# Row blocks combined as they come, joins of inverses in alternating places of the array, squares of keys from a diagonal

## The chip, the cores and the metric

The kernel runs on one core of a Trainium2 chip. The metric is the device time of one execution in microseconds (us), the median of several executions. Lower is better.

## The reference

One decoder block on `x` of 1024 tokens by 1024 channels, all in float32. The normalized input is multiplied by one wide weight `w_in` and split. Two branches follow, then an output product and an MLP:

```python
# gated DeltaNet branch, 8 heads of 128
qkv = silu(causal_short_conv(g_qkv, conv_w))
gq, gk = l2_normalize(q) * 128 ** -0.5, l2_normalize(k)      # k / sqrt(sum(k * k) + EPS)
lhs = strictly_lower(k_beta @ k.T * decay) + eye             # per chunk
sol = triangular_solve(lhs, [v * beta, k_beta * exp(g_cum)])
state = scan over chunks                                     # recurrence per head
...
# attention branch: an indexer selects 256 keys for each query, softmax over them
merged = sigmoid(gate_a) * o_gdn + sigmoid(gate_b) * o_att
x = x + merged @ w_out
h2 = rms_norm(x, norm_mlp_g)
x = x + square(relu(h2 @ w_mlp_up)) @ w_mlp_down             # 1024 -> 4096 -> 1024
```

## The kernel before

**Order.** All work is written as generators that a small planner on the host (`Weave`, line 2003) interleaves. A generator yields None (wait for its own last operation), a key such as `("ss", tb)` (an event that `wv.done` sets) or an engine's letter (until that engine is free by the planner's costs). The planner takes the ready generator with the lowest priority number and so fixes the order of instructions on each engine; an engine then runs its list in that order. Priority 9 is the filler: `gdense` (dense products of `w_in`, line 721), later `wout` and `mlp`. All instructions are recorded through one helper, so the profile puts them on line 2114; tiles tell them apart. Matmuls of plain float32 have two records each (two passes); transposes and products of the rounded float32r halves have one.

**DeltaNet stage.** The tokens form 8 blocks of 128 and a head's matrices have 8 blocks `b`. `keys(h)` (line 820) needs the squared length of each key. `squares` (line 910) gets it so: TensorE transposes four blocks of `kt` into a PSUM tile `tt`, ScalarE squares each with a sum over its row (tile `gj`); twice for 8 blocks. Then come the root (`rsq_w`, three Newton steps on VectorE), the factors `ck`, and for each half four products of keys with themselves, each scaled by `ck` and by the decay `es` in one VectorE operation (tile `am`). GpSimd inverts the 32x32 diagonal blocks. `join(h)` (line 946) puts the inverses together: small matmuls of 32x32 and then 64x64, each placed in a part of the array by `tile_position=(row, column)`, into a PSUM tile `jj`, with ScalarE copies in between. There are four groups of them for a head: 16 and 24 matmuls of 32x32, then 8 and 8 of 64x64. `scan(h)` (line 1044) follows.

**Between attention and MLP.** Attention goes through row blocks in the order 0, 7, 1, 6, 2, 3, 5, 4, two groups of heads each. `wout` multiplies a merged block by `w_out`, `residual` (line 1397) adds `x`, stores the block and sums its squares. The MLP multiplies in a seven-product scheme over two halves of the rows and two halves of the channels. Its first two products of a column pair, p1 and p2, need the normalized rows of blocks 0 to 3 (`norm2`, line 1424), the other five need sums and differences with blocks 4 to 7 (`norm2b`, line 1587, which transposes them in `columns` and splits them in `rounded`). Eight products p1 and p2 of 12 matmuls stand at the head of the order of products (`SEQ`, line 1501).

Of the kernel before, what the change touches and what calls it, by code (L numbers as in the profile page):

```python
# [9 lines left out]
F32 = mybir.dt.float32  # L10
# [4 lines left out]
AF = mybir.ActivationFunctionType  # L15
# [35 lines left out]
def body(tc, a, out, dbg=None):  # L51
# [48 lines left out]

    def rsq_w(pl, dst, src, n, tag):
        t = pl.tile([P, n], F32, name=tag + "t")
        V_.tensor_scalar(dst.bitcast(I32), src.bitcast(I32), -0.5, float(0x5F3759DF), op0=OP.mult, op1=OP.add)
        for _ in range(3):
            yield
            V_.scalar_tensor_tensor(t, dst, -0.5, src, op0=OP.mult, op1=OP.mult)
            yield
            V_.tensor_tensor(t, t, dst, op=OP.mult)
            yield
            V_.scalar_tensor_tensor(dst, t, 1.5, dst, op0=OP.add, op1=OP.mult)  # L110
# [709 lines left out]
    def keys(h):  # L820
# [12 lines left out]
        kss = gp.tile([P, NB], F32, name="kss", bufs=2)  # L833
        yield from squares(kt, kss)
        yield dma
        for b in range(NB):
            A_.activation(es[:, b, :], es[:, b, :], AF.Abs, bias=ngc[:, b, h:h + 1])
            if b % 2:
                yield
            if b % 4 == 3:  # L840
                A_.activation(es[:, b - 3:b + 1, :], es[:, b - 3:b + 1, :], AF.Exp, scale=-1.0)
        rk = gp.tile([P, NB], F32, name="rk", bufs=2)
        ke = gp.tile([P, NB], F32, name="ke", bufs=2)
# [12 lines left out]
        V_.scalar_tensor_tensor(nb_, ck, -1.0, eg[:, :, h], op0=OP.mult, op1=OP.mult)  # L856
        for half in range(2):
            yield tt.ready
            ps, slot_ = tt.get()
            for i in range(4):  # L860
                b = half * 4 + i
                PE_.matmul(ps[:, i, :], blk(kt, b), blk(kt, b), start=True, stop=True)
            yield
            for i in range(4):
                b = half * 4 + i
                V_.scalar_tensor_tensor(am[:, b, :], ps[:, i, :], ck[:, b:b + 1], es[:, b, :],
                                        op0=OP.mult, op1=OP.mult)
                if i % 2:
                    yield
            tt.free(slot_)  # L870
        for half in range(2):
# [74 lines left out]
    def join(h):  # L946
# [8 lines left out]
        ys = am[:, :, 96:128]  # L955
        yp = pj_.tile([P, NB, 32], F32, name="jj")
        for p_ in range(2):
            lo_, hi_ = slice(64 * p_, 64 * p_ + 32), slice(64 * p_ + 32, 64 * p_ + 64)
            for b in range(NB):
                PE_.matmul(yp[lo_, b, :], am[hi_, b, lo_], um[hi_, b, hi_], start=True, stop=True,  # L960
                           tile_position=(64 * p_ + 32, 64 * p_))
        yield
        for p_ in range(2):
            lo_ = slice(64 * p_, 64 * p_ + 32)
            A_.activation(ys[lo_], yp[lo_], AF.Copy)
        yield
        xp = pj_.tile([P, NB, 32], F32, name="jj")
        for p_ in range(2):
            lo_ = slice(64 * p_, 64 * p_ + 32)
# [18 lines left out]
        A_.activation(y6, yp[0:64], AF.Copy)  # L988
        yield
        xp = pj_.tile([P, NB, 64], F32, name="jj")  # L990
        for b in range(NB):
            PE_.matmul(xp[0:64, b, :], t64[0:64, b, :], y6[:, b, :], start=True, stop=True, tile_position=(0, 0))
        yield
        A_.activation(um[0:64, :, 64:128], xp[0:64], AF.Copy, scale=-1.0)
        yield
# [379 lines left out]
    def wout():  # L1375
        yield ("drained", last, 1)
        for idx, (qb, g) in enumerate(ATT):
# [15 lines left out]
            if g:  # L1393
                wv.add(1, residual(qb, pw))
        wv.done("wout")
# [18 lines left out]
    def norm_out(half, k, ps, ring, slot_):  # L1414
# [6 lines left out]
        wv.done("h2k", half, k)  # L1421


    def norm2():
        for tb in range(4):
            yield ("ss", first * 4 + tb)
        bs = slice(first * 4, first * 4 + 4)
        V_.tensor_scalar(nms[:, bs], nss[:, bs], 1.0 / D, EPS, op0=OP.mult, op1=OP.add)
        yield
        yield from rsq_w(cst, nr[:, bs], nms[:, bs], 4, "n2")  # L1430
        yield
        for tb in range(4):
            yield ("xd", first * 4 + tb)
        for c in range(2):
            ys = [x1[first * 4 + i][:, c * HALF:(c + 1) * HALF] for i in range(4)]
            for i in range(4):
                V_.tensor_scalar(ys[i], ys[i], nr[:, first * 4 + i:first * 4 + i + 1], None, op0=OP.mult)
            yield
            for k in range(4 * c, 4 * c + 4):
                ring = (ss, ptr)[k % 2]  # L1440
                yield ring.ready
                ps, slot_ = ring.get()
                for i in range(4):
                    PE_.transpose(ps[:, i * P:(i + 1) * P], ys[i][:, (k % 4) * P:(k % 4 + 1) * P], ident)
                wv.add(1, norm_out(first, k, ps, ring, slot_))

    wv.add(1, kprep())
# [32 lines left out]
    wv.run(until=("pv", NA - 2))  # L1480
    wv.add(2, norm2())

# [91 lines left out]
    def up_low(q, p, x_, o, t):  # L1574
# [5 lines left out]
        if p == UP[-1]:  # L1580
            wv.done("rfree", q)

    comb = {}

    def norm2b():
        half = 1 - first
        for tb in range(4):
            yield ("ss", half * 4 + tb)  # L1590
        bs = slice(half * 4, half * 4 + 4)
        V_.tensor_scalar(nms[:, bs], nss[:, bs], 1.0 / D, EPS, op0=OP.mult, op1=OP.add)
        yield
        yield from rsq_w(cst, nr[:, bs], nms[:, bs], 4, "n2")
        yield

        yt = [hpair(n, F32) for n in ("hh6", "hh7")]
        y22 = [yt[i // 2][:, i % 2] for i in range(4)]
        for i in range(4):
            tb = half * 4 + i  # L1600
            o, src, r = y22[i], x1[tb][:, HALF:], nr[:, tb:tb + 1]
            if i % 2:
                A_.activation(o, src, AF.Copy, scale=r)
            else:
                V_.tensor_scalar(o, src, r, None, op0=OP.mult)
        wv.add(0, columns(0, y22))
        yield
        part = lambda h, c: [x1[4 * h + i][:, c * HALF:(c + 1) * HALF] for i in range(4)]
        t1, t4, t3, t2 = part(first, 0), part(first, 1), part(half, 0), part(half, 1)
        yield ("T", 0, 3)  # L1610
        for i in range(4):
            V_.scalar_tensor_tensor(t1[i], t3[i], nr[:, half * 4 + i:half * 4 + i + 1], t1[i], op0=OP.mult, op1=OP.subtract)
        yield
        for i in range(4):
            V_.tensor_tensor(t2[i], y22[i], t1[i], op=OP.subtract)
        yield
        wv.add(0, columns(2, t2))
        yield ("col", 2)
        for i in range(4):
            V_.scalar_tensor_tensor(t3[i], t3[i], nr[:, half * 4 + i:half * 4 + i + 1], y22[i], op0=OP.mult, op1=OP.subtract)  # L1620
        yield
        wv.add(1, columns(3, t3))
        yield "V"
        for i in range(4):
            V_.tensor_tensor(t4[i], t4[i], t2[i], op=OP.subtract)
        yield ("col", 3)
        wv.add(1, columns(1, t1))
        yield ("col", 1)
        wv.add(1, columns(4, t4))

    places = {0: 0, 2: 2, 3: 4, 1: 6}

    def columns(m, rows):
# [5 lines left out]
        for k in range(4):  # L1639
            ring = (ss, ptr)[k % 2]  # L1640
            yield ring.ready
            ps, slot_ = ring.get()
            for i in range(4):
                PE_.transpose(ps[:, i * P:(i + 1) * P], rows[i][:, k * P:(k + 1) * P], ident)
            if m < 4 and k % 2 == 0:
                th, tl = (hpair(f"{n}{places[m] + k // 2}") for n in ("hh", "hl"))
                for i in range(2):
                    comb[m, k + i] = th[:, i], tl[:, i]
            wv.add(0 if m in (0, 2) else 3, rounded(m, k, ps, ring, slot_))
        wv.done("col", m)  # L1650
# [534 lines left out]
```

## Time and profile before

| | |
|---|---|
| median of 3 runs | 1824.97 us (1824.21 to 1825.02) |
| the profiled execution | 1824.57 us |
| its span, first to last instruction | 1822.9 us |
| TensorE busy | 1807.4 us, 99% |
| VectorE, ScalarE, GpSimd busy | 1266.2, 1036.2, 525.5 us |
| granted TensorE clock | 1.000 |

The span is the profiled execution less 1.67 us around it. An engine's busy time is the union of its instructions; a matmul's record lasts longer than the time until the next one starts, because matmuls are pipelined, so what a matmul costs in a stream is read from the starts.

### The profile page before, as it was taken

The numbers are of one execution on the slowest core, as the hardware profiler recorded it, in microseconds if no ns is written. First come the engines' busy times: TensorE is split into PE (matmuls) and PEld (weight loads), VectorE is DVE, ScalarE is ACT, GpSimd is POOL, SyncE is SP. The second block draws the span as 40 slices with busy tenths as digits, with TensorE's granted clock in tenths as the row PEclk, the third lists the DMA queues.
The fourth block names the chain that finished last, engine by engine and source line by source line (L and its number), as shares of the span: only waits on it lengthen the run. The fifth ranks groups of instructions, "written<-read, shape, count | busy, mean of one in ns | idle before, by whom it ended". The sixth has DMA issues, their size and how long they took to land. (4 is left out here: it accounts for less than half of the span.)

```text
span 1822.9 us, 28546 instructions
## 1 busy us (share of the span) xinstructions
PE 1807.4 (99%) x10316; PEld 1542.0 (85%) x10316; DVE 1266.2 (69%) x2626; ACT 1036.2 (57%) x2273; POOL 525.5 (29%) x738
## 2 busy tenths in 40 slices
PE   9999999999999999999999999999999999999999
PEld 8999998888888888888887888887888888888887
DVE  5556768857777869764448767687766668969673
ACT  6566657765776545445337656576676664343331
POOL 0003530733461724245013111221323322222230
PEclk9999999999999999999999999999999999999999
DMA  4111242132222222231356222224535459473331
GB/s 163 48 47 47 71 128 64 49 97 76 57 58 54 78 70 62 69 84 35 98 168 208 89 77 74 73 89 149 195 136 165 147 173 347 149 249 126 102 133 55
DMA packets 192192, 198.80 MB, mean 109 GB/s; under 512 B 36737, under 2 KB 140466, under 8 KB 192050
## 3 DMA queue, kind: packets, MB, share of 16 engines
q1 hardware_dynamic: 192050, 196.97, 34.2%
q8 instruction: 81, 1.33, 0.3%
q14 instruction: 61, 0.50, 0.1%
HBM read 141.20 MB, written 55.74 MB: 108 GB/s over the span
## 5 line engine op out<-in xcount | busy, mean ns | idle before, releaser
L2114 PE MATMUL dd<-hh,w 128*128 128x512 f32 x1568 | 518.0, 402 | 0.0
L2114 PEld LDWEIGHTS dd<-hh,w 128*128 128x128 f32 x1568 | 288.2, 189 | 50.6
L2114 PE MATMUL dd<-hl,w 128*128 128x512 f32 x784 | 316.1, 403 | 0.9 <-DVE hl L2114 0.9
L2114 ACT ACTIVATE m<-m 128x512 fp32r<-128x512 f32 (+1 forms) x240 | 139.9, 625 | 80.1 <-PE o L2114 30.5
L2114 PE MATMUL dd<-w,hh 128*128 128x256 f32 x960 | 179.4, 284 | 0.4 <-DVE w L2114 0.4
L2114 PE MATMUL dd<-hh,m 128*128 128x512 f32 x520 | 172.1, 396 | 1.0 <-DVE w L2114 0.8
L2114 PEld LDWEIGHTS dd<-hl,w 128*128 128x128 f32 x784 | 147.8, 189 | 26.6 <-DVE hl L2114 1.4
L2114 DVE TENSOR_TENSOR m<-m,m 128x512 fp32r<-128x512 f32 (+2 forms) x184 | 139.4, 784 | 40.8 <-ACT m L2114 35.5
L2114 PEld LDWEIGHTS dd<-w,hh 128*128 128x128 f32 x960 | 151.5, 191 | 1.5 <-DVE w L2114 0.6
L2114 PE MATMUL dd<-w,hl 128*128 128x256 f32 x480 | 136.2, 284 | 0.0
L2114 POOL TENSOR_TENSOR sx<-sx,stmp 128x60 f32<-128x60 f32 (+24 forms) x248 | 110.1, 444 | 19.4
L2114 PEld LDWEIGHTS dd<-hh,m 128*128 128x128 f32 x520 | 96.7, 188 | 20.6 <-DVE w L2114 2.4
L2114 DVE TENSOR_SCALAR_CACHE_REDUCE tkeq<-sc,cand 128x384 f16<-128x384 f32 (+3 forms) x128 | 103.3, 807 | 1.1
L2114 POOL TENSOR_TENSOR m<-m,m 128x512 f32<-128x512 f32 x48 | 67.9, 1421 | 123.5 <-ACT m L2114 60.3
L2114 PE MATMUL dd<-hl,m 128*128 128x512 f32 x260 | 102.3, 393 | 0.9 <-POOL hl L2114 0.9
L2114 POOL TENSOR_TENSOR stmp<-sx,um 128x60 f32<-128x60 f32 (+24 forms) x186 | 79.2, 426 | 64.7 <-DMA um<-ZA 51.1
L2114 ACT ACTIVATE hh<-m 128x1024 fp32r<-128x1024 f32 x44 | 45.2, 1056 | 88.7 <-PE s L2114 41.5
L2114 ACT ACTIVATE ha<-m 128x1024 fp32r<-128x1024 f32 x44 | 45.4, 1056 | 87.7 <-PE s L2114 34.1
L2114 PEld LDWEIGHTS dd<-w,hl 128*128 128x128 f32 x480 | 91.7, 191 | 0.6
L2114 DVE TENSOR_TENSOR w<-w,w 128x1024 fp32r<-128x1024 f32 (+1 forms) x60 | 67.6, 1130 | 33.4 <-ACT w L2114 32.8
L2114 ACT ACTIVATE tkcm<-sc,cand 128x896 f16<-128x896 f32 x64 | 69.9, 1091 | 25.7 <-DVE cand L2114 22.1
L2114 PE MATMUL o<-hh,m 128*128 128x512 f32 x248 | 80.2, 391 | 0.0
(412 smaller groups left out, 4435.4 us busy)
## 6 DMA issues: line engine op xcount, KB each, us to landing
HD<-m SPq DMA_DIRECT2D x112, 256.0 KB, 2.5
m<-HD SPq DMA_DIRECT2D x56, 512.0 KB, 3.9
w<-in_w_in_dram SPq DMA_DIRECT2D x48, 512.0 KB, 3.9
m<-in_w_mlp_up_dram SPq DMA_DIRECT2D x33, 512.0 KB, 5.2
wraw<-in_w_in_dram SPq DMA_DIRECT2D x8, 1024.0 KB, 5.2
m<-in_w_mlp_down_dram SPq DMA_DIRECT2D x16, 512.0 KB, 6.8
w<-in_x_dram SPq DMA_DIRECT2D x10, 512.0 KB, 4.5
es<-GC SPq DMA_DIRECT2D x8, 512.0 KB, 4.6
```

The costliest lines, as they stand in the source:

```text
L2114: ins = f(*args, **kw)
```

## The change

Three parts. **Squares:** `keys` no longer calls `squares`. Each product of keys with themselves has the squared lengths on its diagonal; VectorE multiplies it with the identity and sums the row (one `tensor_tensor_reduce` for each block, its product thrown into `am`), then one operation for each half multiplies by the decay, and after the root one operation multiplies all 8 blocks by `ck`. **Joins:** the small matmuls are issued block by block, so that neighbours lie in different places, and odd blocks write another column place of the array (and other PSUM partitions) than even ones; the copies are split into even and odd blocks. **Row blocks:** `norm2` takes blocks 0 to 2 and block 3 apart; `early` and `early_columns` combine, transpose and split blocks 5 to 7 before `wout` has ended; `norm2b` handles block 4 alone, and `last_columns` transposes its four column parts into one PSUM tile. Roots are taken without gaps (`apart=False`), and `residual` gets priority -1.

```diff
 def keys(h):
-        yield from squares(kt, kss)
         yield dma
...
-        V_.tensor_scalar(ke, kss, 4 * EPS, None, op0=OP.add)
-        yield
-        yield from rsq_w(gp, rk, ke, NB, "rk")
...
         for half in range(2):
             hs = slice(half * 4, half * 4 + 4)
...
-                V_.scalar_tensor_tensor(am[:, b, :], ps[:, i, :], ck[:, b:b + 1], es[:, b, :],
-                                        op0=OP.mult, op1=OP.mult)
+                V_.tensor_tensor_reduce(out=am[:, b, :], in0=ps[:, i, :], in1=ident, op0=OP.mult, op1=OP.add,
+                                        scale=1.0, scalar=0.0, accum_out=kss[:, b:b + 1])
+            V_.tensor_tensor(am[:, hs, :], ps, es[:, hs, :], op=OP.mult)
...
+        V_.tensor_scalar(ke, kss, 4 * EPS, None, op0=OP.add)
+        yield
+        yield from rsq_w(gp, rk, ke, NB, "rk")
...
+        V_.tensor_tensor(am, am, ck[:, :, None].to_broadcast([P, NB, P]), op=OP.mult)
 def join(h):
-        for p_ in range(2):
-            lo_, hi_ = slice(64 * p_, 64 * p_ + 32), slice(64 * p_ + 32, 64 * p_ + 64)
-            for b in range(NB):
-                PE_.matmul(yp[lo_, b, :], am[hi_, b, lo_], um[hi_, b, hi_], start=True, stop=True,
-                           tile_position=(64 * p_ + 32, 64 * p_))
+        for b in range(NB):
+            for p_ in range(2):
+                lo_, hi_, c_ = slice(64 * p_, 64 * p_ + 32), slice(64 * p_ + 32, 64 * p_ + 64), 64 * p_ + 32 * (b % 2)
+                PE_.matmul(yp[c_:c_ + 32, b, :], am[hi_, b, lo_], um[hi_, b, hi_], start=True, stop=True,
+                           tile_position=(64 * p_ + 32, c_))
...
-            A_.activation(ys[lo_], yp[lo_], AF.Copy)
+            for e in range(2):
+                lo_, c_ = slice(64 * p_, 64 * p_ + 32), 64 * p_ + 32 * e
+                A_.activation(par(ys[lo_], e), par(yp[c_:c_ + 32], e), AF.Copy)
...
-        for p_ in range(2):
-            lo_ = slice(64 * p_, 64 * p_ + 32)
-            for b in range(NB):
+        for b in range(NB):
+            for p_ in range(2):
+                lo_ = slice(64 * p_, 64 * p_ + 32)
                 PE_.matmul(xp[lo_, b, :], t64[lo_, b, 0:32], ys[lo_, b, :], start=True, stop=True,
                            tile_position=(64 * p_, 64 * p_))
-        for b in range(NB):
-            PE_.matmul(xp[32:64, b, :], ys[0:32, b, :], t64[0:32, b, 0:32], start=True, stop=True,
-                       tile_position=(0, 32))
+                if not p_:
+                    PE_.matmul(xp[32:64, b, :], ys[0:32, b, :], t64[0:32, b, 0:32], start=True, stop=True,
+                               tile_position=(0, 32))
...
         for b in range(NB):
-            PE_.matmul(yp[0:64, b, :], am[64:128, b, 0:64], um[64:128, b, 64:128], start=True, stop=True,
-                       tile_position=(64, 0))
+            c_ = 64 * (b % 2)
+            PE_.matmul(yp[c_:c_ + 64, b, :], am[64:128, b, 0:64], um[64:128, b, 64:128], start=True, stop=True,
+                       tile_position=(64, c_))
...
+                PE_.matmul(xp[c_:c_ + 64, b, :], t64[0:64, b, :], y6[:, b, :], start=True, stop=True,
+                           tile_position=(0, c_))
 def wout():
-                wv.add(1, residual(qb, pw))
+                wv.add(-1, residual(qb, pw))
+def early(tbs):
+        yield from roots(tbs)
+        for tb in tbs:
...
+            A_.activation(y22[i], y22[i], AF.Copy, scale=r)
+            yield ("turned", 0)
+            V_.scalar_tensor_tensor(b11, b12, r, b11, op0=OP.mult, op1=OP.subtract)
+            V_.scalar_tensor_tensor(b12, b12, r, y22[i], op0=OP.mult, op1=OP.subtract)
+            wv.done("combined", i)
+def early_columns():
+        for j in js:
+            yield ("combined", j)
+        yield ("wo", NA - 2)
+        for m in (0, 2):
...
+                for j in js:
+                    PE_.transpose(ps[:, j * P:(j + 1) * P], y22[j][:, k * P:(k + 1) * P], ident)
+                wv.add(2, early_rounded(m, k, ps, ring, slot_))
+wv.add(8, norm2())
+for tbs in (EARLIER[1:], EARLIER[:1]):
+        wv.add(2, early(tbs))
+wv.add(2, early_columns())
 def norm2b():
...
-        for i in range(4):
-            tb = half * 4 + i
-            o, src, r = y22[i], x1[tb][:, HALF:], nr[:, tb:tb + 1]
...
-        wv.add(0, columns(0, y22))
...
-        wv.add(0, columns(2, t2))
+        tb = ATT[-1][0]
+        yield from roots([tb])
+        V_.tensor_scalar(y, t2[i], r, None, op0=OP.mult)
+        yield ("early",)
+        wv.add(0, last_columns(0, i, y))
...
+        wv.add(0, last_columns(2, i, t2[i]))
...
+        yield ("T", 2, 3)
         wv.add(1, columns(3, t3))
```

## Rows read from the trace of the kernel before

**Rows 1.** The page, part 1 (engines) and part 2 (granted clock).

```profile
PE 1807.4 (99%) x10316; PEld 1542.0 (85%) x10316; DVE 1266.2 (69%) x2626; ACT 1036.2 (57%) x2273; POOL 525.5 (29%) x738
...
PEclk9999999999999999999999999999999999999999
```

**Rows 2.** Busy time by stretch: start:end, length, each engine's busy us and instructions.

```profile
260.00:936.00 676.00, 676.00 (x4263) 571.13 (x4262) 469.70 (x1202) 387.59 (x1055) 248.22 (x547) 1.00 0.26 71
...
1180.00:1246.00 66.00, 62.17 (x325) 51.12 (x324) 54.20 (x92) 45.31 (x91) 15.54 (x12) 1.00 0.24 78
1246.00:1500.00 254.00, 254.00 (x1123) 210.31 (x1122) 168.68 (x251) 171.07 (x333) 75.36 (x52) 1.00 0.50 170
```

**Rows 3.** Instructions by tile, kt and oo: x count: duration ns, first and last start.

```profile
L2114 ACT ACTIVATE kt<-cu,vecs x8: 1138/1151/1169, 266.2 to 772.8; 128x1024 f32<-128x1024 f32 x8
...
L2114 PE MATMUL oo<-svn,es x128: 270/275/275, 391.2 to 927.9; 128*128 128x128 f32 x128
...
L2114 PE MATMUL dd<-hh,w x1568: 387/393/504, 17.2 to 969.8; 128*128 128x512 f32 x196
```

**Rows 4.** Timeline of TensorE, a group of transposes for squares: start, us, instruction.

```profile
470.95 0.60 PE L2114 MATMUL tt<-ident,kt 128*128 128x128 f32 x4
471.31 0.48 PE L2114 MATMUL dd<-hl,w 128*128 128x512 f32 x1
471.62 0.39 PE L2114 MATMUL dd<-hh,w 128*128 128x512 f32 x1
```

**Rows 5.** Timeline of TensorE in the join of head 0.

```profile
377.70 1.09 PE L2114 MATMUL jj<-um,am 32*32 32x32 f32 x32
...
380.53 1.00 PE L2114 MATMUL jj<-am,t 32*32 32x32 f32 x29
...
381.40 0.19 PE L2114 MATMUL jj<-t,am 32*32 32x32 f32 x1
381.40 0.19 PE L2114 MATMUL jj<-am,t 32*32 32x32 f32 x1
381.43 0.19 PE L2114 MATMUL jj<-t,am 32*32 32x32 f32 x1
381.43 0.19 PE L2114 MATMUL jj<-am,t 32*32 32x32 f32 x1
381.46 0.57 PE L2114 MATMUL jj<-t,am 32*32 32x32 f32 x13
...
384.45 1.14 PE L2114 MATMUL jj<-um,am 64*64 64x64 f32 x16
```

**Rows 6.** Groups on VectorE, 260 to 940 us: busy, mean ns, idle before.

```profile
L2114 DVE SCALAR_TENSOR_TENSOR am<-tt,ck,es 128x128 f32<-128x128 f32 x64 | 19.1, 342 | 18.6 <-PE tt L2114 18.6
...
L2114 DVE TENSOR_TENSOR es<-tt,es 128x512 f32<-128x512 f32 x16 | 11.0, 688 | 6.7 <-PE tt L2114 3.5 <-POOL stmp L2114 3.2
...
L2114 DVE TENSOR_TENSOR vv<-vv,fo 128x1024 f32<-128x1024 f32 x8 | 9.8, 1227 | 0.2
```

**Rows 7.** Groups on VectorE, 941 to 1180 us (attention).

```profile
L2114 DVE DVE_READ_ACCUMULATOR2_ANT mx<- 128x1 f32 x96 | 8.0, 83 | 0.0
...
L2114 DVE CUSTOM_DVE_ANT_0 pr<-s,mk 128x128 f32<-128x128 f32 x16 | 4.5, 288 | 2.7 <-PE s L2114 2.5
```

**Rows 8.** Groups on ScalarE, 260 to 940 us.

```profile
L2114 ACT ACTIVATE gj<-tt 128x128 bf16<-128x128 f32 x128 | 35.6, 278 | 15.2 <-PE tt L2114 12.2
...
L2114 ACT ACTIVATE am<-jj 32x256 f32<-32x256 f32 x16 | 6.0, 376 | 10.3 <-PE jj L2114 10.2
```

**Rows 9.** Timeline of TensorE between wout and the MLP; in brackets idle and releaser.

```profile
1213.87 1.07 PE L2114 MATMUL s<-ident,hh 128*128 128x128 f32 x4 [0.59 <-DVE hh L2114]
1214.77 0.60 PE L2114 MATMUL pt<-ident,hh 128*128 128x128 f32 x4
...
1232.95 0.66 PE L2114 MATMUL pt<-ident,w 128*128 128x128 f32 x4 [0.86 <-DVE hl L2114]
...
1240.19 0.63 PE L2114 MATMUL s<-ident,w 128*128 128x128 f32 x4 [1.24 <-DVE hl L2114]
```

More of the change, by code (lines that the diff above doesn't have):

```diff
@@ L991, in join @@
         for b in range(NB):
-            PE_.matmul(xp[0:64, b, :], t64[0:64, b, :], y6[:, b, :], start=True, stop=True, tile_position=(0, 0))
+            c_ = 64 * (b % 2)
+            PE_.matmul(xp[c_:c_ + 64, b, :], t64[0:64, b, :], y6[:, b, :], start=True, stop=True,
+                       tile_position=(0, c_))
         yield
-        A_.activation(um[0:64, :, 64:128], xp[0:64], AF.Copy, scale=-1.0)
+        for e in range(2):
+            A_.activation(par(um[0:64, :, 64:128], e), par(xp[64 * e:64 * e + 64], e), AF.Copy, scale=-1.0)
         yield
@@ L1421, in norm_out, with roots @@
         wv.done("h2k", half, k)
-    def norm2():
[L1425 to L1428, printed above, removed]
+    def roots(tbs):
+        for tb in tbs:
+            yield ("ss", tb)
+        bs = slice(min(tbs), max(tbs) + 1)
+        V_.tensor_scalar(nms[:, bs], nss[:, bs], 1.0 / D, EPS, op0=OP.mult, op1=OP.add)
+        yield from rsq_w(cst, nr[:, bs], nms[:, bs], len(tbs), "n2", apart=False)
+        yield
+    def norm2():
+        tbs = [qb for qb, g in ATT if g and qb // 4 == first]
+        for now in (tbs[:3], tbs[3:]):
+            yield from roots(now)
+            for tb in now:
+                yield ("xd", tb)
+                for c, eng in enumerate("VA"):
+                    yc = x1[tb][:, c * HALF:(c + 1) * HALF]
+                    yield eng
+                    if c:
+                        A_.activation(yc, yc, AF.Copy, scale=nr[:, tb:tb + 1])
+                    else:
+                        V_.tensor_scalar(yc, yc, nr[:, tb:tb + 1], None, op0=OP.mult)
         yield
[L1430 to L1433, printed above, removed]
         for c in range(2):
             ys = [x1[first * 4 + i][:, c * HALF:(c + 1) * HALF] for i in range(4)]
-            for i in range(4):
-                V_.tensor_scalar(ys[i], ys[i], nr[:, first * 4 + i:first * 4 + i + 1], None, op0=OP.mult)
-            yield
             for k in range(4 * c, 4 * c + 4):
@@ L1445, in norm2 @@
                 wv.add(1, norm_out(first, k, ps, ring, slot_))
+            yield
+            wv.done("turned", c)
+    part = lambda h, c: [x1[4 * h + i][:, c * HALF:(c + 1) * HALF] for i in range(4)]
+    y22, comb, pairs = {}, {}, {}
+    places = {0: 0, 2: 2, 3: 4, 1: 6}
+    def early(tbs):
+        yield from roots(tbs)
+        for tb in tbs:
+            i, r = tb % 4, nr[:, tb:tb + 1]
+            b11, b12 = part(first, 0)[i], part(1 - first, 0)[i]
+            y22[i] = part(1 - first, 1)[i]
+            yield ("xd", tb)
+            yield "A"
+            A_.activation(y22[i], y22[i], AF.Copy, scale=r)
+            yield
+            yield ("turned", 0)
+            yield "V"
+            V_.scalar_tensor_tensor(b11, b12, r, b11, op0=OP.mult, op1=OP.subtract)
+            yield "V"
+            V_.scalar_tensor_tensor(b12, b12, r, y22[i], op0=OP.mult, op1=OP.subtract)
+            yield
+            wv.done("combined", i)
@@ new lines, in early_columns @@
+    def early_columns():
+        js = [tb % 4 for tb in EARLIER]
+        for j in js:
+            yield ("combined", j)
+        yield ("wo", NA - 2)
+        for m in (0, 2):
+            if m:
+                yield
+                for j in js:
+                    yield "V"
+                    V_.tensor_tensor(y22[j], y22[j], part(first, 0)[j], op=OP.subtract)
+                yield
+            for k in range(4):
+                if k % 2 == 0:
+                    pairs[m, k // 2] = [hpair(f"{n}{places[m] + k // 2}") for n in ("hh", "hl")]
+                    for i in range(2):
+                        comb[m, k + i] = [t[:, i] for t in pairs[m, k // 2]]
+                ring = (ss, ptr)[k % 2]
+                yield ring.ready
+                ps, slot_ = ring.get()
+                for j in js:
+                    PE_.transpose(ps[:, j * P:(j + 1) * P], y22[j][:, k * P:(k + 1) * P], ident)
+                wv.add(2, early_rounded(m, k, ps, ring, slot_))
+        yield
+        wv.done("early")
@@ L1447, in body, with early_rounded @@
+    def early_rounded(m, k, ps, ring, slot_):
+        cs = slice(min(EARLIER) % 4 * P, (max(EARLIER) % 4 + 1) * P)
+        hi, lo = (t[:, cs] for t in comb[m, k])
+        yield 0.2
+        yield "A"
+        A_.activation(hi, ps[:, cs], AF.Copy)
+        yield
+        yield "V"
+        V_.tensor_tensor(lo, ps[:, cs], hi.bitcast(F32), op=OP.subtract)
+        ring.free(slot_)
+    EARLIER = sorted(qb for qb, g in ATT[:-1] if not g and qb // 4 != first and qb != ATT[-1][0])
     wv.add(1, kprep())
@@ L1629, in norm2b, with last_columns @@
         wv.add(1, columns(4, t4))
-    places = {0: 0, 2: 2, 3: 4, 1: 6}
+    def last_columns(m, i, row):
+        yield ss.ready
+        ps, slot_ = ss.get()
+        for k in range(4):
+            PE_.transpose(ps[:, k * P:(k + 1) * P], row[:, k * P:(k + 1) * P], ident)
+        yield
+        for kk in range(2):
+            src = ps[:, kk * 2 * P:(kk + 1) * 2 * P].rearrange("p (a b) -> p a b", a=2)
+            hi, lo = (t[:, :, i * P:(i + 1) * P] for t in pairs[m, kk])
+            A_.activation(hi, src, AF.Copy)
+            yield
+            V_.tensor_tensor(lo, src, hi.bitcast(F32), op=OP.subtract)
+            if kk:
+                ss.free(slot_)
+            yield
+            wv.done("T", m, 2 * kk)
+            wv.done("T", m, 2 * kk + 1)
     def columns(m, rows):
@@ L1648, in columns @@
                     comb[m, k + i] = th[:, i], tl[:, i]
[L1649 removed]
+            wv.add(3, rounded(m, k, ps, ring, slot_))
         wv.done("col", m)
```

81 lines of the change are left out of this document (33 added, 48 removed).

## The prediction

> **What bounds the kernel now.** The page comes first: TensorE is busy 1807.4 of 1822.9 us and no other engine passes 69% [rows 1]. A busy engine may still run slowly, so the clock is next: it is granted in full, 2.4 GHz, in all 40 slices [rows 1]. Then the table by stretch. From 260 to 936 us, the DeltaNet stage, TensorE has no idle time at all, and neither has it from 1246 to 1500 us, in the MLP; there 254 us hold 1123 matmuls of 512 columns, one each 0.226 us [rows 2]. Between them, from 1180 to 1246 us, 3.8 us are idle [rows 2]. So the end moves by what TensorE no longer has to do, and by what of those 3.8 us goes; work on VectorE or ScalarE counts only where a matmul comes to wait for it.
>
> One thing has to hold for that: the DeltaNet stage must be paced by the stream of products and not by the chain of a head (convolution, keys, inverse on GpSimd, join, scan). The eight convolutions of keys start from 266.2 to 772.8 us; the last scan ends near 928 us, while dense products are left until 969.8 us [rows 3]. The heads follow the products that feed them, and behind the last scan there is still some filler. If the products come earlier, the last head starts earlier by as much, and its chain keeps the cover it has.
>
> **Squares of keys.** Removed: for each head two groups of four transposes, 16 groups in all. What one costs is read in the stream: the group starts at 470.95 us, the next product at 471.31, and the one behind that at 471.62 [rows 4]. That is 0.36 us, and the product behind it takes 0.31 in place of 0.23 us: 0.44 us for a group, 16 x 0.44 = **7.0 us**. ScalarE loses 64 squares of 278 ns [rows 8] with their reads of the sum.
>
> VectorE gets more. Eight scalings of 342 ns become eight reductions from PSUM; the nearest rows are the same kind of instruction in attention, 288 ns with a read of 83 ns [rows 7], so 8 x 0.03 = 0.2 us more. Two multiplications by the decay come on top, 688 ns each as for queries, and one of 128x1024 by a factor spread over columns, 1227 ns as in the output [rows 6]: 1.4 + 1.2 = 2.6 us. Together 2.8 us a head, 22 us in all, on an engine that was busy 470 of 676 us in that stretch [rows 2]; it would be at 75%. I cost it at nothing, because between the steps of keys TensorE has dense products to run. The root now stands behind the products in place of ahead of them; the two PSUM tiles are freed after the reductions and the multiplication, some 0.9 us later than before, and queries, values and output share their ring. If that cover were gone, a late `tt` tile holds up the transposes behind it in TensorE's order, up to 0.9 us for each of 16 halves, 14 us.
>
> **Joins.** The same number of matmuls is issued, so only their spacing can change. In one place, records of 32x32 start 32 ns apart: 13 last 0.57 us and one 0.19, (0.57 - 0.19) / 12 [rows 5]. Where the order passes from one place to another, records of both run side by side, for a few records only: two start at 381.40 and two at 381.43 us, 16 ns a record [rows 5]. So places that differ in rows and columns do work at once, if neighbours in the order lie in different places; before, 16 records of one place come in a row. From the first start to the last, the four groups of a head take 1.09 - 0.19 = 0.90 us (32 records), 381.46 + 0.38 - 380.53 = 1.31 us (48 records), and, with the same 0.19 us for a record of 64x64, 1.14 - 0.19 = 0.95 us twice (16 records, 63 ns each) [rows 5].
>
> After the change the first group goes around four places, the second around three. At 16 ns a record, which is what the rows show, they take 31 x 16 = 0.50 and 47 x 16 = 0.75 us: 0.40 and 0.56 us less. The bounds: nothing less, if the order feeds a place no faster than now, and 8 ns with four places at once, 0.25 and, with three, 0.51 us, that is 0.65 and 0.80 less. The two groups of 64x64 alternate between places that have the same rows and differ in columns. No row shows such a pair at work at once. The bounds are nothing and half of 0.95 us; I take 0.35 of that 0.47 us, as two places at once is what the rows with other rows show, short of the full half because the first and last records have no partner. A head gives 0.40 + 0.56 + 0.35 + 0.35 = 1.66 us, eight heads **13.3 us** (0 to 8 x 2.39 = 19 us).
>
> A rule of the Trainium skill stands against half of this. "TensorE: Matmul & The Clock Gate", Part 3, What overlaps and what doesn't, says that a weight load overlaps a matmul in flight only when its row group differs; by it the 64x64 groups would keep their pace and the sum of all parts would be 16.8 us instead of 22.4. "TensorEngine Tiling (Array Packing)", Key Properties, says that different tiles load weights and multiply in parallel, with no such limit. The rows show overlap across row groups and are silent on places that share one.
>
> ScalarE's copies are split: two of 32x256 elements, 376 ns each [rows 8], and two of 64x512 become twice as many of half the size, an estimated 0.7 us a head (128 elements a row take 278 ns in the squares) on an engine that loses more than 2.2 us of squares. The join waits for each copy a little longer; between the four groups TensorE runs dense products, so I cost it at nothing.
>
> **Row blocks.** The number of transposes stays at 32 for products 0 and 2 of the scheme. What changes is when they can run. Before, the first four wait for a row of `y22` (0.59 us idle) and then take 0.90 us, from 1213.87 to 1214.77 [rows 9], where four transposes cost 0.44 [rows 4], because each waits for its own row: 0.46 us more. Later transposes wait twice for the split of an earlier one on VectorE, 0.86 and 1.24 us [rows 9]. Together 3.15 us, most of the 3.8.
>
> Afterwards blocks 5 to 7 are combined and transposed while `wout` and the first eight products run, and those eight are 96 matmuls of 0.226 us, 21.7 us of cover. What is left behind the last `wout` is a chain for block 4: residual, square, one root, one scaling, some 16 operations before four transposes. None of the sizes in question takes more than the 1.23 us of a 128x1024 operation [rows 6], most are tiny, so that even 16 x 1.23 = 20 us would fit into that cover. So the first loss, 0.59 + 0.46 = 1.05 us, goes. The two waits of 0.86 and 1.24 us come from VectorE being behind the planner's costs in products 3, 1 and 4 of the scheme; these steps now come earlier but on an engine that has five roots instead of two to take, eleven small operations each, and the same splits. I let half of them go, 1.05 us. Sum: **2.1 us**; bounds: 3.15 us and a loss of 2 us, if the additional small operations hold up the attention's last splits or the operands of the first products by as much as the waits there now. Priority -1 of the residual moves one operation ahead by less than a microsecond; cost nothing.
>
> **Sum.** 7.0 + 13.3 + 2.1 = 22.4 us. The profiled execution took 1824.57 us, 0.4 below the median: 1824.6 - 22.4 = 1802.2 us, and as a median of runs 1802.5 us.
>
> **Rivals.**
> - *Places that share rows don't work at once.* The 64x64 groups stay at 0.95 us. In the second 32x32 group two of three places share rows, so 32 of its records go one by one at 32 ns, 1.0 us, 0.3 less than now; the first still has two row groups, 0.40 less. 0.70 x 8 = 5.6 us from joins, 1824.6 - 7.0 - 5.6 - 2.1 = 1810 us. For it speaks that every overlap in the trace is one of different rows; against it nothing in the trace. The rule on weight loads of the Trainium skill's "TensorE: Matmul & The Clock Gate", cited above, would come out here.
> - *The joins gain nothing* (the change doesn't do there what it says): the order feeds TensorE no faster than one record in 32 ns. Then 1824.6 - 9.1 = 1815.5 us. Against it speak the pairs at 16 ns [rows 5], for it that these last only a few records.
> - *All places at once*: 19 us from joins and all of 3.15 us, 1824.6 - 29.2 = 1795.4 us.
> - *Slower.* VectorE's additional work reaches TensorE. The place is `tt`: the ring has two tiles, they are held longer, and the transposes and products behind stand in TensorE's fixed order. The gain of 22.4 us is used up when each of the 16 halves holds TensorE by 1.4 us; the work in one half is 4 reductions and a multiplication, 4 x 0.37 + 0.69 = 2.2 us against 4 x 0.34 = 1.4 before, so that the wait would have to exceed all of the 0.8 us added, and dense products would have to be missing at each. With 2 us at each half: 1824.6 - 22.4 + 32 = 1834 us. Against it speaks that TensorE had no idle time at all in this stage, though scaling on VectorE had waited for `tt` 18.6 us in all [rows 6]: VectorE waits for TensorE there, not the other way round.
>
> **How the numbers follow.** Forecast (1797 to 1807) 0.57, shared rows (1810) 0.18, no gain in joins (1815.5) 0.11, all places at once (1795) 0.07, waits that use up part or all of the gain 0.07, of which more than half end slower. The likeliest gives 1802.5 us. The range of 8 in 10 takes in all places at once with a microsecond to spare at one end, shared rows with the loss of 2 us and more in the row blocks at the other: 1794 to 1814 us, with 0.82 of the chances; left out are no gain in joins and waits. The likeliest case alone has 1797 to 1807. A change of 0.2%, 3.6 us, is about what can be told from none. Faster by more: 0.93; within it 0.03; slower 0.04.
>
> **What would show it.** Squares: 64 records of `tt<-ident,kt` in place of 128, and no rise of TensorE's idle time before 936 us. Joins: 32x32 records of one group some 16 ns apart, the first group lasting 0.7 and not 1.09 us, a group of 64x64 0.8 and not 1.14 us; if 64x64 stays at 1.14, places that share rows take turns. Row blocks: no idle time ahead of the first transposes of products 0 and 2, and some 1.7 in place of 3.8 us idle around the start of the MLP. The prediction is wrong if TensorE's idle time grows by more than some 3 us anywhere, or if the stretch from the first convolution of keys to the last dense product shortens by much less than 20 us.

## The result, and the profile after

The changed kernel takes 1807.31 us (1806.61 to 1808.67) beside 1824.81 for the kernel before on the same chip, a ratio of 0.991 (95% interval 0.9895 to 0.9922): 17.5 us faster, where 22.4 were forecast. That is inside the range, but partly by luck: the sum hides two large errors of opposite sign, and the profile shows both.

Page of the profile after, parts 1 and 2, and busy time by stretch, moved by 16 us against [rows 2] so that the same work stands in a line (start:end, length, each engine's busy time and instructions, granted clock, DMA share, GB/s):

```profile
PE 1783.6 (99%) x10252; PEld 1517.6 (84%) x10252; DVE 1287.2 (71%) x2746; ACT 1022.8 (57%) x2186; POOL 533.3 (30%) x738
...
PEclk9999999999999999999999999999999999999999
```

```profile
260.00:920.00 660.00, 659.71 (x4252) 553.83 (x4250) 486.83 (x1309) 373.78 (x965) 255.04 (x547) 1.00 0.28 76
920.00:1164.00 244.00, 238.78 (x1269) 199.10 (x1268) 179.99 (x511) 159.28 (x315) 57.72 (x43) 0.99 0.33 106
1164.00:1230.00 66.00, 60.11 (x294) 48.97 (x293) 49.89 (x91) 40.37 (x87) 14.31 (x10) 0.97 0.31 104
1230.00:1484.00 254.00, 254.00 (x1122) 210.39 (x1121) 171.24 (x250) 172.14 (x336) 75.32 (x52) 1.00 0.49 164
```

The stretch from 936 to 1180 us of the kernel before, which stands against the second line:

```profile
936.00:1180.00 244.00, 242.44 (x1288) 202.54 (x1287) 173.69 (x494) 153.80 (x307) 55.26 (x41) 1.00 0.36 116
```

The page alone looks as it did [rows 1]. The DeltaNet stage still has next to no idle TensorE (0.3 us), with VectorE at 74%. But from 1164 to 1230 us 5.9 us are idle, where 3.8 were [rows 2], ahead of that 5.2, where 1.6 were, and the clock is no longer full in either stretch.

**Joins.** Timeline of TensorE in the join of head 0; of the second group (48 records in all) the first and the last record:

```profile
369.71 0.45 PE L2203 MATMUL jj<-um,am 32*32 32x32 f32 x32
...
372.13 0.21 PE L2203 MATMUL jj<-am,t 32*32 32x32 f32 x1
...
372.64 0.19 PE L2203 MATMUL jj<-am,t 32*32 32x32 f32 x1
...
374.80 0.68 PE L2203 MATMUL jj<-um,am 64*64 64x64 f32 x16
...
377.01 0.68 PE L2203 MATMUL jj<-am,t 64*64 64x64 f32 x16
```

With 0.19 us for one record, first to last start is 0.26, 0.51, 0.49 and 0.49 us, where [rows 5] gave 0.90, 1.31, 0.95 and 0.95: 2.36 us a head, **18.9 us** in eight. That is the upper bound of the prediction, 19, and not its 13.3. A 64x64 record starts every 0.49 / 15 = 33 ns in place of 63, although all 16 use the same rows of the array.

**Squares.** From each start to the next, the 128 records of `tt<-ident,kt` took 12.1 us before, and the 64 that are left take 5.7: 6.3 us. That leaves out the product behind a group, whose longer time the forecast of 7.0 had counted. The whole stretch has it in: by tile, the convolutions of keys and the dense products after the change (x count: duration ns, first and last start):

```profile
L2203 ACT ACTIVATE kt<-cu,vecs x8: 1139/1147/1168, 264.8 to 746.9; 128x1024 f32<-128x1024 f32 x8
L2203 PE MATMUL dd<-hh,w x1568: 387/392/501, 15.9 to 942.6; 128*128 128x512 f32 x196
```

From the first convolution to the last dense product it is 677.8 us, where it was 703.6 [rows 3]: **25.8 us** less. Without the 18.9 of the joins, **6.9 us** are left for the squares.

**Given back.** 18.9 + 6.9 = 25.8 us; only 17.5 arrived. Timelines of TensorE and then of VectorE and ScalarE at the end of attention (in brackets idle time and what ended it):

```profile
1139.94 0.49 PE L2203 MATMUL pt<-ident,pr 128*128 128x128 f32 x3
1143.54 0.84 PE L2203 MATMUL pt<-ident,pr 128*128 128x128 f32 x5 [3.11 <-ACT pr L2203]
...
1144.61 1.05 PE L2203 MATMUL dd<-hh,m 128*128 128x512 f32 x2
```

```profile
1137.19 0.20 DVE L2203 TENSOR_SCALAR nm<-mx 128x1 f32<-128x1 f32 x1
1137.32 0.17 DVE L2203 TENSOR_SCALAR nms<-nss 128x2 f32<-128x2 f32 x1
1137.52 1.22 DVE L2203 TENSOR_SCALAR nr<-nms 128x2 int32<-128x2 int32 x1
...
1142.38 0.16 DVE L2203 SCALAR_TENSOR_TENSOR nr<-n2t,nr 128x3 f32<-128x3 f32 x1
1142.46 0.16 DVE L2203 RECIPROCAL mx<-nm 128x1 f32<-128x1 f32 x1
```

```profile
1142.65 0.83 ACT L2203 ACTIVATE pr<-pr,mx 128x640 f32<-128x640 f32 x1 [1.40 <-DVE mx L2203]
```

Read upwards: TensorE waits for a row of probabilities, ScalarE scales it when the reciprocal is there, and ahead of the reciprocal VectorE has 22 small operations in a row, two roots of eleven, from 1137.32 to 1142.46 us. One of them takes 1.22 us in place of 0.16. Timeline of GpSimd at that time:

```profile
1137.41 1.29 POOL L2203 TENSOR_TENSOR sg<-sg,m 128x512 f32<-128x512 f32 x1
```

It ends at 1138.70, the small operation at 1138.74, so it looks held by it for that time; every operation of these roots that takes over 0.4 us in this kernel, in E7 and in E9, twelve in all, ends within 0.05 us of one of GpSimd. The second large gap, 3.24 us ahead of the transposes of block 4, on TensorE and on VectorE:

```profile
1188.51 1.09 PE L2203 MATMUL s<-ident,hh 128*128 128x128 f32 x4 [3.24 <-DVE hl L2203]
```

```profile
1180.49 0.14 DVE L2203 TENSOR_SCALAR nms<-nss 128x1 f32<-128x1 f32 x1
...
1183.45 0.16 DVE L2203 SCALAR_TENSOR_TENSOR nr<-n2t,nr 128x1 f32<-128x1 f32 x1
...
1187.82 0.55 DVE L2203 TENSOR_TENSOR hl<-s,hh 128x384 fp32r<-128x384 f32 x1
```

The transposes need a tile of ring `s` (two PSUM tiles in turn), and it comes free with the last split of the early columns. Ahead of that split stand the root of block 4 (again with one held operation) and 4.2 us of other work. Idle time from 1136 to 1230 us is 9.4 us in seven gaps; in the same work of the kernel before it was 3.5 in four. Behind each large gap the clock falls, as the table by 10 us shows:

```profile
1140.00:1150.00 10.00, 6.89 (x31) 5.49 (x29) 5.33 (x20) 6.90 (x14) 1.29 (x1) 0.83 0.21 73
1150.00:1160.00 10.00, 10.00 (x61) 8.51 (x58) 6.91 (x21) 6.05 (x12) 3.94 (x3) 1.00 0.00 0
1180.00:1190.00 10.00, 6.76 (x36) 5.59 (x35) 7.98 (x20) 7.68 (x22) 4.15 (x3) 0.92 0.00 1
1190.00:1200.00 10.00, 10.00 (x44) 8.15 (x43) 7.26 (x14) 5.71 (x13) 1.99 (x2) 0.91 0.15 55
```

Ten products of 512 columns start 0.427 us apart in place of 0.227 there (1.2 and 2.4 GHz): 2.0 us. The transposes and products at the edges of these stretches lose another 1.2 us. With the 5.9 us of idle time that is 9.1 us, and 25.8 - 9.1 = 16.7. The profiled executions differ by 18.0 us (1824.57 and 1806.61); 1.4 us of that are there at the first convolution already (266.2 and 264.8 us), a point that executions of the kernels below reach at 264.9 to 266.3 us. 16.7 + 1.4 = 18.1.

### The profile page after: what moved, and what is told of

Read it like the earlier page. It is cut to its first block, busy times and chain, and to the rows that moved or that the text cites. A ratio compares the mean times of both kernels' runs of the same rounds, so it can differ in the third digit from the quotient of the medians.

```text
span 1804.9 us, 28444 instructions
## 1 busy us (share of the span) xinstructions
PE 1783.6 (99%) x10252; PEld 1517.6 (84%) x10252; DVE 1287.2 (71%) x2746; ACT 1022.8 (57%) x2186; POOL 533.3 (30%) x738
## 4 chain that ended last, share of the span: by engine, by line
PE 93%; DVE 4%; ACT 1%; issue 1%; POOL 1%; DMA 0%; SPq 0%; ACTq 0%; POOLq 0%; DVEq 0%
PE dd L2203 55%; PE o L2203 15%; PE s L2203 7%; PE pt L2203 6%; PE tt L2203 3%; PE cc L2203 2%; PE sq L2203 2%; PE oo L2203 1%; PE jj L2203 1%; DVE w L2203 1%; DVE hl L2203 1%; DVE m L2203 0%; PE tp L2203 0%; DVE n2t L2203 0%; DMA pj<-in_x_dram 0%
## 5 line engine op out<-in xcount | busy, mean ns | idle before, releaser
L2203 ACT ACTIVATE m<-m 128x512 f32<-128x512 f32 (+1 forms) x240 | 139.9, 625 | 79.3 <-PE dd L2203 34.3
L2203 DVE TENSOR_TENSOR m<-m,m 128x512 fp32r<-128x512 f32 (+2 forms) x184 | 143.3, 804 | 38.7 <-ACT m L2203 33.3
L2203 POOL TENSOR_TENSOR sx<-sx,stmp 128x60 f32<-128x60 f32 (+24 forms) x248 | 119.7, 483 | 19.4
L2203 POOL TENSOR_TENSOR stmp<-sx,um 128x60 f32<-128x60 f32 (+24 forms) x186 | 83.4, 448 | 89.5 <-DMA um<-ZA 61.8
L2203 ACT ACTIVATE tkcm<-sc,cand 128x896 f16<-128x896 f32 x64 | 70.0, 1094 | 28.3 <-DVE cand L2203 25.2
L2203 ACT ACTIVATE w<-w 128x1024 fp32r<-128x1024 f32 x48 | 50.8, 1058 | 53.9 <-PE dd L2203 53.7
```

Of the source, the lines that this page charges most:

```text
L2203: ins = f(*args, **kw)
```

## The experiments

**E1, E2, E3: one part alone; E4: two parts.** Each takes its lines of the diff and leaves the rest of the kernel before as it was. Of each the line that marks it:

```diff
 E1, E4  +  PE_.matmul(yp[c_:c_ + 64, b, :], ..., tile_position=(64, c_))
 E2, E4  +  V_.tensor_tensor_reduce(out=am[:, b, :], in0=ps[:, i, :], in1=ident, ..., accum_out=kss[:, b:b + 1])
 E3      +  wv.add(2, early(tbs))                 # with it: roots without gaps, residual at priority -1
```

> The kernel before with the new order and places of the joins alone. Theory A (places that share rows work at once, as the starts of the records in the changed kernel read: 19.6 to 8.1 us for 32x32 and 17.1 to 9.8 us for 64x64, first start to last, over eight heads): 18.8 us less, 1824.8 - 18.8 = 1806.0 us. Theory B (the sum of the prediction): 13.3 us less, 1811.5 us. Theory C (places that share rows take turns): 5.6 us less, 1819 us.

> The kernel before with the squares of keys from the diagonal of their product alone. Both theories, A and B: 16 groups of four transposes at 0.40 to 0.44 us gone, 6.4 to 7.0 us less, 1817.8 to 1818.4 us, and no idle time of TensorE from 260 to 930 us. Rival: the longer hold of the two tt tiles costs TensorE something when the joins keep their old length; then 1820 us or more, with gaps ahead of tt groups.

> The kernel before with the row blocks of the second half combined as they come, the roots without gaps and the residual's priority, and nothing else. Theory A (the loss of some 8 us between the last dense product and the MLP comes from this part): 1824.8 + 8 = 1833 us, with two idle stretches of TensorE of about 3 us and half clock behind each. Theory B (the sum of the prediction): 2.1 us less, 1822.7 us. Theory C (the loss arises only together with the shorter joins, for instance because loads of weights are then late): no loss here, 1822 to 1825 us.

> The kernel before with joins and squares and without the row blocks. Theory A: 18.8 + 7.0 = 25.8 us less, 1799 us, so 8 us faster than the changed kernel. Theory B: 20.3 us less, 1804.5 us. Theory C (what is gained early is lost in the attention whatever the row blocks do, because something there can't come earlier): the same 1807 us as the changed kernel.

Measured: E1 1820.0 us (0.9973, 0.9962 to 0.9985), E2 1832.4 (1.0045, 1.003 to 1.006), E3 1832.4 (1.0046, 1.0031 to 1.0061), E4 1799.2 (0.9864, 0.9849 to 0.9878), beside 1824.5.

E3 and E4 answer as theory A said: the row blocks cost 7.9 us alone and 1807.3 - 1799.2 = 8.1 us on top of the others, and joins with squares gain 25.2. Theories B and C fall for both, though in E3's profile only the second of the two gaps has half clock behind it. In E1 and E2 the joins alone gain 4.5 us and the squares alone lose 8. By their times alone E1 would be theory C's (1819 us) and E2 its rival's (1820 us or more), but neither reason is there. Their own records are as short as in E4 (18.9 us and 6.3 us from start to start), and E2 has no gaps ahead of `tt` groups: TensorE is busy 676.00 of 676 us from 260 to 936 us. What differs is the order of the rest. In E4 the order of TensorE's instructions, from the last scan to the end, is that of the kernel before, 4232 records in a row, only 25.8 us earlier at the first and 24.5 at the last of them. In E1 and E2 the planner, which sees other costs in the DeltaNet stage, has written another one. Busy time by stretch in E1:

```profile
260.00:936.00 676.00, 675.94 (x4366) 568.68 (x4365) 481.43 (x1251) 401.57 (x1116) 254.57 (x550) 1.00 0.29 79
936.00:1180.00 244.00, 238.69 (x1258) 197.59 (x1257) 169.27 (x466) 152.15 (x298) 55.27 (x43) 1.00 0.34 106
1180.00:1246.00 66.00, 57.56 (x275) 46.97 (x274) 45.31 (x77) 37.02 (x72) 10.81 (x8) 0.95 0.15 50
```

8.4 us are idle from 1180 to 1246 us, where 3.8 were [rows 2], at a clock of 0.95. From 250 us on, gaps of over 0.25 us add up to 12.8 us in E1 and 13.2 in E2, 4.7 in the kernel before, and the clock falls to half twice in E1 and three times in E2. So a part alone isn't measured by undoing the others here: each edit deals the order behind it anew. Both came out 14 us slower than their share, most of it in those gaps and behind them.

**E5: the places by themselves.** E4 with other places and the same order and copies.

```diff
-            c_ = 64 * (b % 2)
+            c_ = 0                      # both groups of 64x64
-                lo_, hi_, c_ = ..., 64 * p_ + 32 * (b % 2)
+                lo_, hi_, c_ = ..., 64 * p_      # first group of 32x32
```

> Joins and squares without row blocks (1799.2 us), with every 64x64 join in one place again and the first 32x32 group in two places (other rows and other columns) in place of four; the order of all instructions, the copies and their count stay. Theory A (places that share rows and differ in columns work at once, and that is what the joins gained more than forecast): the two 64x64 groups go back from 0.47 to 0.95 us from first start to last, 2 x 0.48 x 8 = 7.7 us, the first 32x32 group from 0.28 to 0.5 us, 1.8 us, together 1808 to 1809 us. Theory C (the gain of the joins came from the order of neighbours or the split copies alone, places with the same rows take turns): no more than 1.8 us, 1799 to 1801 us.

1808.5 us (0.9913, 0.9897 to 0.993): theory A, 9.3 us slower than E4. Timeline of TensorE in the join of head 0:

```profile
370.47 0.69 PE L2126 MATMUL jj<-um,am 32*32 32x32 f32 x32
...
375.80 1.14 PE L2126 MATMUL jj<-um,am 64*64 64x64 f32 x16
...
378.46 1.14 PE L2126 MATMUL jj<-am,t 64*64 64x64 f32 x16
```

Only the column place of every other record was changed, and with it the PSUM partitions that it writes and the copies read, and 0.68 became 1.14 us again. The order of all 10252 records is the same. Two places with other rows give (0.69 - 0.19) / 31 = 16 ns a record, four give 8.4.

**E6, E7, E8: ways to the late reciprocal.** The changed kernel with the roots in steps (E6), with the norm and the early blocks given to the planner later (E7), and with a cost of small operations in the planner that is nearer to the trace (E8; 22 took 5.1 us, 0.23 each).

```diff
 E6  -        yield from rsq_w(cst, nr[:, bs], nms[:, bs], len(tbs), "n2", apart=False)
 E6  +        yield from rsq_w(cst, nr[:, bs], nms[:, bs], len(tbs), f"n2{min(tbs)}")
 E7  +    wv.run(until=("p", NA - 1, 3))        # ahead of wv.add(8, norm2())
 E8  -   return wv.issue(name, ins, 0.07 + n / 960, 0.12, ...)                                     # VectorE
 E8  +   return wv.issue(name, ins, max(0.07 + n / 960, 0.24 if wv.shared else 0), 0.12, ...)
```

> The changed kernel with the roots of the second norm in steps again, each chain with its own small tile, so that other VectorE work can go between. Theory A1 (22 small operations in a row stand ahead of the reciprocal of the last attention block, and that makes the idle stretch of 3.1 us and the half clock behind it): that stretch goes, 1807.3 - 3.1 - 1.6 = 1802 to 1803 us, and the second stretch of 3.2 us at the transposes of block 4 stays. Theory B1 (VectorE as a whole is late there, whatever the order): the stall appears a little later, 1806 us or more.

> The changed kernel with the norm and the early row blocks handed to the planner only when the last row of probabilities has been planned. Theory A1: no root ahead of the reciprocal, the first idle stretch of 3.1 us goes, 1802 to 1803 us. Theory B1: roots and scalings that come later make the operands of the first products late, and a stretch of idle time of 2 us or more appears ahead of the first transposes of rows of x, 1806 us or more.

> The changed kernel with one number of the planner changed: in attention and MLP an operation of VectorE costs it 0.24 us at least (a small operation of a root takes 0.235 us from start to start in the trace; the plan had 0.07). Theory A2 (both stretches of about 3 us come from roots that the plan takes for three times shorter than they are): both shrink to under 1 us and the clock stays full, 1797 to 1800 us. Theory A1 alone: only the first goes, 1802 to 1803 us. Theory B1: another order with as much idle time, 1806 us or more.

E6 1818.4 us (0.9966, 0.9953 to 0.9979), E7 1806.0 (0.99, 0.9885 to 0.9914), E8 1804.3 (0.9892, 0.9878 to 0.9907).

In E7 the gap at the probabilities is down to 0.97 us, and another comes 12 us later: the root of one block stands ahead of the residual that frees a tile of `dd`, and three of its operations take 1.2 us, while GpSimd has four operations end to end (1152.84 to 1157.82 us). TensorE and VectorE:

```profile
1159.47 0.80 PE L2204 MATMUL dd<-hh,m 128*128 128x512 f32 x1 [4.21 <-DVE w L2204]
```

```profile
1154.25 1.15 DVE L2204 TENSOR_TENSOR n2t<-n2t,nr 128x1 f32<-128x1 f32 x1
1155.43 1.19 DVE L2204 SCALAR_TENSOR_TENSOR nr<-n2t,nr 128x1 f32<-128x1 f32 x1
1156.66 1.19 DVE L2204 SCALAR_TENSOR_TENSOR n2t<-nr,nms 128x1 f32<-128x1 f32 x1
...
1158.73 1.28 DVE L2204 TENSOR_TENSOR w<-w,dd 128x512 f32<-128x512 f32 x2
```

In E8 no gap is over 1.8 us and the clock stays full, but its gaps of over 0.25 us, from 250 us on, add up to 9.7 us, 10.9 in the changed kernel: a truer cost made the large waits small and left most of their sum. A1 holds for the place of the first gap, B1 for what became of it (E7's 1806.0 is B1's time, E8's lies between); A2 falls for the sum. E6 fits nothing: its gaps add up to 4.3 us, fewer than the 4.7 of the kernel before, and yet it is 11 us slower than the changed kernel.

**E9, E12: what made E6 slow.** In E6 each chain of a root has a tile of its own, and everything allocated behind them on the left half of memory is moved, by 160 bytes if each of the five new tiles takes 32 (no view shows addresses). Busy time of E6 by stretch, one in the first half of the MLP, one in the second:

```profile
1230.00:1484.00 254.00, 254.00 (x1095) 205.62 (x1094) 165.66 (x246) 166.47 (x324) 74.47 (x51) 1.00 0.48 161
1600.00:1700.00 100.00, 100.00 (x443) 82.81 (x442) 78.26 (x69) 37.69 (x38) 24.35 (x9) 1.00 0.51 172
```

At full clock and with no idle time, a product takes 254 / 1095 = 0.232 us in the first stretch, where it took 0.226 [rows 2], and 100 / 443 = 0.226 in the second. In the first, operands come from both halves (`hh` left, most of `m` right), in the second from the left alone. E9 keeps E6's steps and moves nothing.

```diff
+    n2t = cst.tile([P, 8], F32, name="n2t")          # E9: 32 bytes, as the tile before; E12: [P, 32] under a new name
-        yield from rsq_w(cst, nr[:, bs], nms[:, bs], len(tbs), f"n2{min(tbs)}")
+        yield from rsq_w(cst, nr[:, bs], nms[:, bs], len(tbs), "n2", n2t[:, bs])
```

> The kernel with the roots in steps (1818.4 us) with one edit: its chains share one tile of 32 bytes, a column for each block, in place of a tile each, so that no tile behind them is moved; there the left half of memory had moved by 160 bytes against the right half, and products of 512 columns took 0.232 us in place of 0.226 in the MLP and from 260 us on, at full clock. Theory P (the place of operands in memory is what cost that time): products of operands on both halves are back at 0.226 us, 1799 to 1802 us, and what is left shows the roots in steps: idle time of about 4.3 us in place of 10.9, so that the row blocks cost 0 to 2 us more than leaving them out (1799.2). Rival (the order of the roots, or a state of the chip, made the products slower): 1816 to 1820 us again.

E9: 1799.1 us (0.9861, 0.9846 to 0.9875), 19.3 us faster than E6 with the same order of TensorE's 10252 records. Its two stretches:

```profile
1230.00:1484.00 254.00, 254.00 (x1122) 210.31 (x1121) 172.94 (x252) 175.17 (x336) 78.48 (x54) 1.00 0.49 166
1600.00:1700.00 100.00, 100.00 (x443) 82.81 (x442) 74.27 (x68) 36.22 (x36) 23.78 (x9) 1.00 0.44 146
```

So E6's test of theory A1 is read from E9. Timeline of VectorE there:

```profile
1137.99 0.19 DVE L2202 TENSOR_SCALAR nms<-nss 128x2 f32<-128x2 f32 x1
1138.21 1.22 DVE L2202 TENSOR_SCALAR nr<-nms 128x2 int32<-128x2 int32 x1
...
1139.82 0.16 DVE L2202 RECIPROCAL mx<-nm 128x1 f32<-128x1 f32 x1
```

Six small operations stand ahead of the reciprocal in place of 22, the first gap is gone, the second is 1.3 us, and the clock is full. The roots in one piece had cost 1807.3 - 1799.1 = 8.2 us.

E12 asks whether any move does it, or where operands lie within 128 bytes; it is E10 (below) with that tile made 128 bytes long.

> The fastest kernel so far (roots in steps in one shared tile, splits of the early columns first, 1797.3 us), with that tile 128 bytes long, under a name of its own, so that the left half of memory moves by 128 bytes against the right half. In the kernel with a tile for each chain it had moved by 160 bytes, and products of 512 columns took 0.232 us. Theory P1 (what counts is where operands lie within 128 bytes): no change, 1797 us, products at 0.226 us. Rival P2 (any move of one half against the other does it): some 18 us more, 1815 us.

```profile
1230.00:1484.00 254.00, 254.00 (x1099) 206.29 (x1098) 164.95 (x244) 170.61 (x332) 75.70 (x52) 1.00 0.48 163
```

1808.7 us (0.9913, 0.9897 to 0.993), 11.4 us slower than E10 with the same order of TensorE's records, 254 us holding 1099 products in place of 1122. P1 falls: a move by 128 bytes costs too. It costs less than 160 did, so P2's "any move, 18 us" isn't the rule either. Which places suit each other stays open.

**E10, E11: a better version.** E10 is E9 with the splits of the early columns first; E11 is E4 with E8's cost.

```diff
 E10 -                wv.add(2, early_rounded(m, k, ps, ring, slot_))
 E10 +                wv.add(-1, early_rounded(m, k, ps, ring, slot_))
```

> As the one before, and the splits of the early columns planned ahead of everything else on VectorE and ScalarE (priority -1 in place of 2). Theory A3 (the transposes of block 4 wait for a place that the last of these splits frees too late): the idle time of 1.3 + 0.5 + 0.7 us there goes, with 1.5 us of half clock behind it: 3 to 4 us less than the one before, 1796 to 1798 us. Rival (VectorE is loaded, and what goes first makes operands of products late instead): the same or more than the one before.

> Joins and squares without row blocks (1799.2 us), with the planner's 0.24 us for small operations of VectorE in attention and MLP. Theory A2 (a plan that knows what a small operation takes leaves less idle time): the 3.5 us from 1154 to 1214 shrink, 1797 to 1798.5 us. Rival (it gives another order of the same quality, as in the changed kernel): 1799 to 1804 us.

E10: 1797.3 us (0.9853, 0.9838 to 0.9867), 1.8 us less than E9, where 3 to 4 were expected; the gap ahead of block 4 is 0.79 us and no longer 1.3 + 0.5 + 0.7, and the 1.5 us of half clock counted with it were not there in E9 to be saved. It is the fastest median, 10 us below the changed kernel; from E4 and E9, 2 us above it, the intervals don't tell it apart. E11: 1805.7 us (0.9898, 0.9882 to 0.9915): another order, with a gap of 2.8 us; the rival's side, and beyond it.

## Why the prediction was right, and where its steps failed

**The bound** held: in the DeltaNet stage the end moves by what TensorE no longer does, and VectorE's additional work, counted at nothing, cost nothing there (659.71 of 660 us busy). The stretch that the prediction named as a sign, from the first convolution of keys to the last dense product, is 25.8 us shorter, where joins and squares were to give 20.3.

**Squares.** Right: 6.9 us for 7.0, as what the joins leave of the 25.8; 6.3 of it are read from the transposes' own starts.

**Joins.** Right in mechanism, too small: 18.9 us, the upper bound, for 13.3. The step that failed is the price of places without a row in the trace. 64x64 gained 0.46 of the possible 0.47 us and not 0.35; four places gave 8.4 ns a record and not 16. The pairs at 16 ns [rows 5] were two places at work, and were taken as the pace of any number. The rival that places with shared rows take turns is refuted by E5; by the rule cited with it, from "TensorE: Matmul & The Clock Gate" of the Trainium skill, Part 3, a 64x64 group would have stayed at 1.14 us, and the measured 0.68 decides against it here.

**Row blocks.** The wrong sign: 2.1 us of gain forecast, 8.1 of loss measured (E3, E4). Two steps failed. The first, "most are tiny, so that even 16 x 1.23 = 20 us would fit into that cover", looked at the chain of block 4 alone; two other roots stood in one piece ahead of the attention's last reciprocal. The bound of 2 us named that very mechanism, additional small operations that hold up the attention's last splits, but priced it by today's waits. As they ran, the 22 operations took 5.1 us, the held one 1.22 of it. The second: no term stood for the clock. Beside E4 the changed kernel's gaps of over 0.25 us add up to 10.9 us and not 6.0, and 3.2 us go to the half clock behind the two large ones: 4.9 + 3.2 = 8.1. E9 shows that roots in steps undo the loss, but the forecast gain isn't there either: its 1799.1 us are E4's 1799.2, and E10's 1797.3 are not told apart from it.

**Sum.** 18.9 + 6.9 - 8.1 = 17.7 in place of 13.3 + 7.0 + 2.1 = 22.4: the joins' 5.6 us more were outweighed by the row blocks' 10.2 us less. The prediction said what would prove it wrong, idle time that grows by over 3 us; it did, by 5.9, and the time fell into the range because the joins paid for it. That these two errors nearly cancelled was luck.

## What to carry to other kernels

A chain of tiny operations that nothing can be put between is one long operation: price it as their sum, with the holds by GpSimd, and look at what stands behind it on its engine. A part of a change in a kernel whose order is planned can't be measured by undoing the others; compare records from start to start, and check that the order behind is the same. Where two kernels differ by a small tile, compare the pace of a long run of equal products before reading anything into their times.

## What the hardware showed that was not expected

- Places of the array with the same rows and other columns work at once: 64x64 records every 33 ns in place of 63; 32x32 records in four places every 8.4 ns, in two every 16 (E5).
- Products of 512 columns with operands on both halves of memory took 0.232 us in place of 0.226 when the left half lay further by what counts as 160 bytes (E6 and E9: 1095 in place of 1122 in 254 us), and 0.231 for 128 bytes (E12: 1099); with both operands on the left they stayed at 0.226. That is 19.3 and 11.4 us of the whole.
- Behind its gaps of 3.1 and 3.2 us the changed kernel ran four to six products of 512 columns at half clock. The length of a gap alone doesn't tell when that happens: in E3 the clock stayed full behind a gap of 3.11 us (1.00 from 1170 to 1180 us), in E8 with gaps of up to 1.7, and in E6 it fell behind three of 1.34, 0.47 and 0.69 us (0.83 from 1210 to 1220 us).
- A small operation of VectorE takes 0.16 us, and up to 1.29 (E9) while GpSimd runs; the long ones end with an operation of GpSimd's. Not every operation of GpSimd's holds one.
